# S5's loads of tables, G1, H and local kernels: issued on SyncE's queue instead of GpSimd's

## The chip, the core and the metric

The kernel runs on one core of a Trainium2 chip. Its engines are TensorE (PE: matmuls, and weight loads as PEld), VectorE (DVE), ScalarE (ACT), GpSimd (POOL) and SyncE (SP, which computes nothing and only issues transfers). Each engine works through its own list of instructions in order; a wait of one instruction holds all that stand behind it on that engine. Transfers between HBM and the core's memory (DMAs) go through queues, one for each issuing engine here, and are moved by 16 DMA engines. The metric is the time of one execution on the device in microseconds (us), lower is better.

## What is computed

A decoder trunk of two layers over 1024 positions with a width of 1024, in float32. The first layer's mixer is a gated DeltaNet; the second layer's is an S5 state-space layer: 64 groups of 16 channels each drive one complex state of 64 dimensions. Each mixer runs beside a cross-attention of 4 heads into 256 memory tokens, and an MLP follows. The change touches only the S5 layer:

```python
def s5_scan(u, abar_re, abar_im, bbar_re, bbar_im, c_re, c_im):
    """h_t = Abar h_{t-1} + Bbar u_t per group; y_t = Re(C h_t)."""
    ...
def s5_mixer(x, w_in, ...):
    u, xq = jnp.split(x @ w_in, [S5_DIM], axis=-1)
    ...
    y = s5_scan(u, abar_re, abar_im, bbar_re, bbar_im, c_re, c_im)
    y = y + d_skip * u
    zg = jax.nn.gelu(y)
    return zg * jax.nn.sigmoid(zg @ w_glu + b_glu), xq

def reference(x, mem, ...):
    for i in range(2):
        mix, xq = gdn_mixer(...) if i == 0 else s5_mixer(...)
        cross = memory_attention(xq, mem, w_kv_mem[i])
        x = layer_norm(DN_ALPHA * x + concatenate([mix, cross]) @ w_o[i])
        x = layer_norm(DN_ALPHA * x + square(relu(x @ mlp_w1[i])) @ mlp_w2[i])
```

## The kernel before

Float32 matmuls are made of three passes: an operand is split into a high part (a cast on ACT) and a low part (a subtraction on DVE), and `mm3` (L383 to L385) multiplies high by high, high by low and low by high. A weight therefore passes through three stations: `load_raw` (L351) loads it on SP into one of the two `raw` buffers, ACT casts it (L362), DVE subtracts (L363), and only then can TensorE use it. `wuh` and `wul` are the two parts of a weight of the S5 input `u`, `wur` its raw load; `wq`, `wv` and `wk` are the attention's weights in the same way. `mem_kv` (L1496) loads the memory tokens by the same raw buffers (`mem`), for the keys and values; ACT casts them at L1510.

The S5 front is the stretch of the second layer in which S5 runs, from about 1310 to 1640 us. It works on 8 rounds m of 8 groups each. A round has these steps:

- `s5_u` (L1967): the projection of the input onto 128 channels, from `xT` (`xTh`, `xTl`) and `wu`; the result is stored on SP to `ud` in HBM (L1978).
- `s5_driving` (L1986): the loads of a round's driving side, for each half round one `G1` (through `s5_load`, L1981) and two tables `tab` (L1997) of 256 KB each.
- `s5_drive` (L2015): loads `u` back from `ud` on SP (L2021), multiplies it by G1 on TensorE (`p1`), and turns and scans the product on DVE and ACT with the two tables; the result is `r`.
- `s5_reading` (L2002): the loads of the reading side: the local kernel `M0` (`s5_local`, L2008, 512 KB from `zd` into a quarter of the buffer `s5t`; the last round's, `ml`, has a buffer of its own and is loaded ahead of the front) and two `H` of 256 KB.
- `s5_read` (L2052): the products `py` of the local kernel with `u` (L2059) and of H with `r` (L2060), then ACT's GELU (`zg`), which SP stores to `yd` (L2063). The GLU reads `yd` after the front.

G1, H, the tables and the local kernels are made earlier, stored to HBM (`g1d`, `h1d`, `tabd`, `zd`), and come back in the front. In the kernel before, GpSimd issues all of these 72 loads: 32 tables, 16 G1, 16 H and 8 local kernels, 21 MB together. All other loads and stores of the front are issued by SP.

The order of the work in the front comes from a string of steps, one for K (keys and values of the memory), U (`s5_u`), D (`s5_drive` with the loads of the round after it and the reading loads of its own), R (`s5_read`), Q, S, T and V (the attention's queries, scores, transposes and values) and G (the GLU):

```python
    FRONT = "K K D0 K K U20 U21 R0 D1 K K U30 U31 R1 D2 K K Q00 U40 U41 R2 D3 Q01 S00 U50 U51 R3 D4 T00 V00 S01 ..."
```

At the end of the build a planner (`settle`, L58) puts all instructions of each engine into an order by estimated costs (`price`, L291; it takes an issue by POOL for dearer than one by SP) and fixes it. So a load that is moved to another engine can stand at another place among its neighbours than it was written at. Buffers come from pools with a fixed count by tag: two `raw`, nine `h2` (the tables), seven `h1` (G1, H and `r`). A load into a buffer waits until its last reader is done.

Each DMA signals its landing on a completion counter. The DMAs of SP use eight counters in turn, those of POOL eight others; a DMA waits until the DMA before it on its counter, the eighth before it on its queue, has landed.

Of the kernel before, what the change touches and what calls it, by code (L numbers as in the profile page):

```python
# [16 lines left out]
P = 128  # L17
# [13 lines left out]
class Trunk:  # L31
# [1948 lines left out]

    def s5_load(self, nm, tag, src):  # L1981
        t = self.tile(tag, [P, 4, P], F32, nm)
        self.nc.gpsimd.dma_start(t, src)
        return t

    def s5_driving(self, m):  # L1986

        out = []
        for b in range(2):
            gs = slice(4 * b, 4 * b + 4)  # L1990
            G1 = self.s5_load("G1", "h1", self.g1d[m, :, gs])
            c, q = (2 * m + b) % 8, m // 4
            tabs = []
            for x in range(2):
                t = self.tile("h2", [P, 4, P], F32, "tab")
                src = self.tabd[1:3, c, q] if x else self.tabd[0, c, q].unsqueeze(0).to_broadcast([2, 64, 4, P])
                self.nc.gpsimd.dma_start(t.rearrange("p g t -> p (g t)"), src.rearrange("k p g t -> k p (g t)"))  # L1997
                tabs.append(t)
            out.append((G1, tabs))
        return out  # L2000
# [7 lines left out]
    def s5_local(self, m, o):  # L2008

        M0 = o.rearrange("p (g x) -> p g x", g=8)  # L2010
        z = self.zd[m]
        self.nc.gpsimd.dma_start(M0, bass.AP(z.tensor, z.offset, [[16, 8], [8 * 240, 16], [240, 8], [1, P]]))
        return M0

    def s5_drive(self, m, loads):  # L2015
# [447 lines left out]
```

## Time and profile before

| what | value |
|---|---|
| time, median of 3 runs | 2501.77 us (2498.99, 2501.77, 2503.67) |
| time of the profiled execution | 2499.32 us |
| its span in the profile | 2497.3 us |
| its TensorE clock, mean granted | 0.998 |
| bytes by SP's queue (q1) | 372.50 MB, 46.9% of 16 engines' span |
| bytes by POOL's queue (q0) | 46.76 MB, 7.1% of 16 engines' span |

The page of the profile gives the busy time of each engine first, then a picture of the span in 40 slices of 62.4 us. These two of its rows show the busy share of TensorE and of the DMA engines in each slice, in tenths:

```profile
PE   9999999999999999999999999999999999999998
...
DMA  6445545566335665587455498884237544573422
```

The S5 front lies in the slices from the 22nd (which begins at 1311 us) to the 27th; the four that show DMA shares of 0.8 and 0.9 begin at 1436 us. A TensorE row is read as line, operation, output and inputs, tile, shape; the time in brackets behind it is how long the engine stood idle just before, and whose end released it. A row of a DMA issue gives the tile, the queue, the number of transfers and their size, and the median time from issue to landing.

### The profile page before, as it was taken

To read this page: it belongs to the slowest core of one execution; us is meant where nothing else is said; L and a number is where in the kernel's file an instruction comes from. 1 tells how busy PE (TensorE), PEld (TensorE's weight loads), DVE (VectorE), ACT (ScalarE), POOL (GpSimd) and SP (SyncE) were. 2 spreads that over 40 slices of the span, in tenths; PEclk is the share of its full clock that TensorE was granted. 3 is DMA by queue.
4 is the path that set the end of the run, shared out by engine and by line. 5 is a ranking of instruction groups with operands and counts; after the bars stand their busy time and mean duration, and the time that the engine had idled before them with its cause. 6 is when DMAs were issued, how large, how long until landed. Compare 5 with 4: busy or idle time off the path is not lost. (4 is left out here: it accounts for less than half of the span.)

```text
span 2497.3 us, 36513 instructions
## 1 busy us (share of the span) xinstructions
PE 2468.7 (99%) x12199; PEld 2056.2 (82%) x12199; DVE 1933.0 (77%) x3661; ACT 1387.5 (56%) x3114; POOL 275.4 (11%) x405
## 2 busy tenths in 40 slices
PE   9999999999999999999999999999999999999998
PEld 7888888888787888888888888888887888888886
DVE  7776868676889987879988856683988655587777
ACT  7766677665557576554444254672466555544444
POOL 1111111110001011312120122200010000000001
PEclk9999999999999999999999999999999999999999
DMA  6445545566335665587455498884237544573422
GB/s 206 131 114 155 153 137 141 150 194 200 109 116 184 212 222 185 177 281 252 136 171 156 139 238 223 198 265 143 77 118 239 173 162 148 205 277 105 148 89 97
DMA packets 304844, 426.17 MB, mean 171 GB/s; under 512 B 132832, under 2 KB 150192, under 8 KB 304656
## 3 DMA queue, kind: packets, MB, share of 16 engines
q1 hardware_dynamic: 270320, 372.50, 46.9%
q0 software_dynamic: 31744, 46.76, 7.1%
q10 hardware_dynamic: 2592, 4.59, 0.5%
q8 instruction: 96, 1.57, 0.3%
q14 instruction: 92, 0.75, 0.1%
HBM read 287.84 MB, written 135.76 MB: 170 GB/s over the span
## 5 line engine op out<-in xcount | busy, mean ns | idle before, releaser
L383 PE MATMUL q<-wkh,hkh 128*128 128x512 f32 x784 | 305.9, 390 | 0.0
L384 PE MATMUL q<-wkl,hkh 128*128 128x512 f32 x784 | 305.7, 390 | 0.0
L385 PE MATMUL q<-wkh,hkl 128*128 128x512 f32 x784 | 305.4, 390 | 0.0
L851 ACT CAST wkh<-wr 128x512 fp32r<-128x512 f32 x168 | 104.8, 624 | 233.2 <-PE q L384 153.6
L383 PEld LDWEIGHTS q<-wkh,hkh 128*128 128x128 f32 x784 | 147.2, 188 | 31.7 <-ACT wkh L851 1.0
L385 PEld LDWEIGHTS q<-wkh,hkl 128*128 128x128 f32 x784 | 147.2, 188 | 30.3
L384 PEld LDWEIGHTS q<-wkl,hkh 128*128 128x128 f32 x784 | 147.2, 188 | 30.3
L852 DVE TENSOR_TENSOR wkl<-wr,wkh 128x512 fp32r<-128x512 f32 x168 | 115.6, 688 | 63.7 <-issue 50.2
L383 PE MATMUL wi<-xTh,wih 128*128 128x512 f32 x376 | 152.0, 404 | 0.0
L384 PE MATMUL wi<-xTl,wih 128*128 128x512 f32 x376 | 150.0, 399 | 0.0
L385 PE MATMUL wi<-xTh,wil 128*128 128x512 f32 x376 | 149.9, 399 | 0.0
L506 POOL TENSOR_TENSOR mv<-mv,mhalf 128x1 f32<-128x1 f32 x32 | 29.5, 922 | 981.0 <-DVE mv L500 936.3
L852 DVE TENSOR_TENSOR hkl<-hr,hkh 128x512 fp32r<-128x512 f32 x196 | 134.0, 684 | 3.3 <-ACT hkh L851 3.3
L851 ACT CAST hkh<-hr 128x512 fp32r<-128x512 f32 x196 | 120.8, 616 | 4.6 <-DMA hr<-hd 4.6
L383 PE MATMUL o<-ow,ok 128*128 128x512 f32 x256 | 101.3, 396 | 1.0 <-ACT ok L1714 1.0
L385 PE MATMUL o<-ow,ok 128*128 128x512 f32 x256 | 101.3, 396 | 0.2
L384 PE MATMUL o<-ow,ok 128*128 128x512 f32 x256 | 100.0, 390 | 0.0
L844 DVE TENSOR_TENSOR y<-q,y 128x512 f32<-128x512 f32 x136 | 88.0, 681 | 0.0
L385 PEld LDWEIGHTS wi<-xTh,wil 128*128 128x128 f32 x376 | 70.8, 188 | 12.7
L383 PEld LDWEIGHTS wi<-xTh,wih 128*128 128x128 f32 x376 | 70.9, 189 | 11.8
L384 PEld LDWEIGHTS wi<-xTl,wih 128*128 128x128 f32 x376 | 71.0, 189 | 11.6
L1714 ACT CAST ok<-os 128x512 fp32r<-128x512 f32 x56 | 34.7, 621 | 53.3 <-PE o L385 39.1
(621 smaller groups left out, 7335.0 us busy)
## 6 DMA issues: line engine op xcount, KB each, us to landing
hr<-hd SPq DMA_DIRECT2D x212, 256.0 KB, 2.8
wr<-in_w_dram SPq DMA_DIRECT2D x56, 512.0 KB, 4.8
hd<-u SPq DMA_DIRECT2D x100, 256.0 KB, 2.2
w1r<-in_w_dram SPq DMA_DIRECT2D x48, 512.0 KB, 3.7
hd<-hid SPq DMA_DIRECT2D x60, 256.0 KB, 2.3
hd<-p SPq DMA_DIRECT2D x60, 256.0 KB, 2.6
w1r<-in_w_dram SPq DMA_DIRECT2D x48, 256.0 KB, 3.4
wir<-in_w_in_dram SPq DMA_DIRECT2D x23, 512.0 KB, 4.8
```

The costliest lines, as they stand in the source:

```text
L383: mm(ps, a[0], b[0], start=start, stop=False, skip_group_check=onto)
L384: mm(ps, a[0], b[1], start=False, stop=False, skip_group_check=onto)
L385: mm(ps, a[1], b[0], start=False, stop=stop, skip_group_check=onto)
L506: nc.gpsimd.tensor_tensor(mv[:, 3:4], mv[:, 2:3], self.mhalf[:, 0:1], op=ALU.pow)
L844: V.tensor_tensor(o, bank[t], o, op=ALU.add)
L851: nc.scalar.copy(hi, s)
L852: nc.vector.tensor_tensor(lo, s, f32(hi), op=ALU.subtract)
L1714: nc.scalar.copy(hi, s)
```

## The change

In three functions `dma_start` is called on `nc.sync` instead of `nc.gpsimd`. Sources, destinations, sizes and buffers are the same.

```diff
     def s5_load(self, nm, tag, src):
         t = self.tile(tag, [P, 4, P], F32, nm)
-        self.nc.gpsimd.dma_start(t, src)
+        self.nc.sync.dma_start(t, src)
         return t
...
     def s5_driving(self, m):
...
-                self.nc.gpsimd.dma_start(t.rearrange("p g t -> p (g t)"), src.rearrange("k p g t -> k p (g t)"))
+                self.nc.sync.dma_start(t.rearrange("p g t -> p (g t)"), src.rearrange("k p g t -> k p (g t)"))
...
     def s5_local(self, m, o):
...
-        self.nc.gpsimd.dma_start(M0, bass.AP(z.tensor, z.offset, [[16, 8], [8 * 240, 16], [240, 8], [1, P]]))
+        self.nc.sync.dma_start(M0, bass.AP(z.tensor, z.offset, [[16, 8], [8 * 240, 16], [240, 8], [1, P]]))
```

The orders of TensorE, VectorE and ScalarE are the same in both kernels. POOL's list is 72 rows shorter, SP's 72 rows longer, and the planner chose where on SP each load stands. Three places of SP's list follow; a row with + is a load that came from POOL, a row without a sign stood there before (source line, output and input, shape; numbers behind a name tell buffers apart).

The first is ahead of the second load of memory tokens (`mem_14936`), at 1416 us, while SP stores and loads rows of `x` for the layer's end. The tables are those of the first three rounds:

```order
 L2366 DMA x_6957<-y_11552 128x1024 x2
+L1997 DMA tab_15017<-tabd 128x1x512
+L1997 DMA tab_15021<-tabd 128x1x512
+L1997 DMA tab_15023<-tabd 128x1x512
+L1997 DMA tab_15072<-tabd 128x1x512
+L1997 DMA tab_15074<-tabd 128x1x512
+L1997 DMA tab_15078<-tabd 128x1x512
+L1997 DMA tab_15080<-tabd 128x1x512
+L1997 DMA tab_15283<-tabd 128x1x512
+L1983 DMA G_2867_15019<-g1d 128x512
 L353 DMA mem_14936<-in_memT_dram 128x1024
```

Nine loads, eight tables and a G1, now stand between the stores of `x` and `mem_14936`, which stood right behind each other.

The second is at 1469 us, between two attention weights (`wvr_15481` and `wvr_15499`). The loads that came are those of the reading side of one round (local kernel and two H) and two G1 of the next:

```order
 L353 DMA wvr_15481<-in_wv_dram 128x1024
+L2012 DMA s5t_14779<-zd 128x8x128
 L2063 DMA yd<-zg_15221 128x512
 L2063 DMA yd<-zg_15233 128x512
+L1983 DMA G_2911_15281<-g1d 128x512
+L1983 DMA G_2914_15287<-g1d 128x512
+L1983 DMA H_2917_15294<-h1d 128x4x128
+L1983 DMA H_2918_15296<-h1d 128x4x128
 L2021 DMA s5t_14779<-ud 128x1024
 L353 DMA wvr_15499<-in_wv_dram 128x1024
```

Five loads now stand ahead of the second attention weight, and the local kernel stands ahead of the two stores of `yd`.

The third follows right behind it (from 1477 us on), up to the loads of the next round. `wqr_15521` is an attention weight, `wur_15556` the weight of `u` of round 4:

```order
 L353 DMA wvr_15499<-in_wv_dram 128x1024
+L1997 DMA tab_15468<-tabd 128x1x512
+L1997 DMA tab_15472<-tabd 128x1x512
+L1997 DMA tab_15474<-tabd 128x1x512
+L1997 DMA tab_15686<-tabd 128x1x512
 L353 DMA wqr_15521<-in_w_in_dram 128x1024
 L1978 DMA ud<-s5t_14779 128x8x128
 L353 DMA wur_15556<-in_w_in_dram 128x1024
 L2063 DMA yd<-zg_15404 128x512
+L2012 DMA s5t_14779<-zd 128x8x128
 L2063 DMA yd<-zg_15416 128x512
+L1983 DMA G_2944_15464<-g1d 128x512
```

Four tables now stand ahead of `wqr` and `wur`; the next round's local kernel, G1 and H stand behind `wur`.

## The prediction

> **What bounds the kernel now.** I read the page's busy times first.
>
> ```profile
> span 2497.3 us, 36513 instructions
> ...
> PE 2468.7 (99%) x12199; PEld 2056.2 (82%) x12199; DVE 1933.0 (77%) x3661; ACT 1387.5 (56%) x3114; POOL 275.4 (11%) x405
> ```
>
> TensorE is busy for 2468.7 of 2497.3 us, so at most 28.6 us of its idle time can be won anywhere. The order of PE, DVE and ACT is unchanged, so the change acts only through when data arrive. The next view is who TensorE waits for between 1360 and 1700 us, where the S5 front runs (line, releaser: us in total, times, longest).
>
> ```profile
> PE wu L383 <- ACT wuh L362: 1.4, 1, 1.4
> ...
> PE wu L383 <- ACT xTh L534: 0.7, 1, 0.7
> PE wu L385 <- DVE wul L363: 0.5, 1, 0.5
> ...
> PE wu L384 <- DVE xTl L535: 0.2, 1, 0.2
> ```
>
> Two places stand out. The first, in order of time of TensorE (start, duration, idle before), is this:
>
> ```profile
> 1504.23 0.39 PE L384 MATMUL wq<-xTl,wqh 128*128 128x512 f32 x1
> 1504.45 0.39 PE L385 MATMUL wq<-xTh,wql 128*128 128x512 f32 x1
> 1506.27 0.50 PE L383 MATMUL wu<-xTh,wuh 128*128 128x512 f32 x1 [1.43 <-ACT wuh L362]
> ...
> 1507.53 0.75 PE L385 MATMUL wu<-xTh,wul 128*128 128x512 f32 x1 [0.52 <-DVE wul L363]
> 1508.08 0.63 PE L383 MATMUL wu<-xTh,wuh 128*128 128x512 f32 x1
> ...
> 1511.29 0.40 PE L385 MATMUL wu<-xTh,wul 128*128 128x512 f32 x1
> 1511.52 0.40 PE L383 MATMUL wu<-xTh,wuh 128*128 128x512 f32 x1
> ```
>
> Matmuls follow each other every 0.22 to 0.23 us at full pace (1504.23 to 1504.45, 1511.29 to 1511.52). From 1504.45 to 1511.29 twelve of these steps take 6.84 us where 12 x 0.227 = 2.72 would do: **4.1 us lost**, half by waiting, half because matmuls behind the wait run at 0.63 us. Why it waited, on ACT and DVE:
>
> ```profile
> 1505.17 1.04 ACT L362 CAST wuh<-wur 128x1024 fp32r<-128x1024 f32 x1 [6.50 <-DMA wur<-in_w_in_dram]
> ...
> 1506.25 1.22 DVE L363 TENSOR_TENSOR wul<-wur,wuh 128x1024 fp32r<-128x1024 f32 x1 [5.35 <-ACT wuh L362]
> ```
>
> A weight load of SP landed late. ACT stood for it for 6.50 us. At full pace TensorE would want `wuh` at 1504.68 and `wul` at 1505.13; `wul` was ready at 1507.47. So that load must land 2.4 us earlier, by about 1502.7, for the whole loss to go.
>
> The second place is at 1430: 0.7 + 0.2 us behind ACT's `xTh`. On ACT:
>
> ```profile
> 1428.15 1.14 ACT L1510 CAST memh<-mem 128x512 fp32r<-128x512 f32 x2 [3.06 <-DMA mem<-in_memT_dram]
> ...
> 1429.67 1.07 ACT L534 CAST xTh<-xt 128x512 fp32r<-128x512 f32 x2
> ```
>
> ACT takes its work in order, and 3.06 us went by on another load of SP (`mem`) just ahead.
>
> **Why those loads are late.** I compare how fast the two issuing paths move data: first while POOL's loads have the DMA engines alone, second SP's alone but for the last 2 us, third both (stretch, ..., granted clock, DMA share, GB/s), with each stretch's main queue (packets, MB) below.
>
> ```profile
> 1413.00:1419.00 6.00, 6.00 (x28) 4.98 (x27) 5.09 (x9) 0.00 (x0) 5.62 (x8) 1.00 0.54 98
> 1439.00:1450.00 11.00, 11.00 (x84) 10.49 (x83) 3.33 (x5) 4.51 (x8) 1.67 (x2) 1.00 0.92 286
> 1470.00:1506.00 36.00, 34.84 (x189) 29.79 (x187) 19.62 (x34) 15.61 (x24) 11.17 (x14) 1.00 1.02 255
> ```
>
> ```profile
> q0 software_dynamic: 1786, 0.57, 53.1%
> q1 hardware_dynamic: 2647, 3.13, 91.8%
> ```
>
> POOL's queue (q0) gets 98 GB/s out of engines that nobody else uses; SP's (q1) gets 286. Together they move 255 with the engines full. So the loads that the change moves are the slow ones, and they hold up SP's. By the page, issue to landing (median us):
>
> ```profile
> tab<-tabd POOLq DMA_DIRECT2D x32, 256.0 KB, 11.9
> ...
> G<-g1d POOLq DMA_DIRECT2D x16, 256.0 KB, 12.5
> ...
> H<-h1d POOLq DMA_DIRECT2D x16, 256.0 KB, 13.4
> ...
> s5t<-zd POOLq DMA_DIRECT2D x7, 512.0 KB, 12.5
> ```
>
> **The change part by part.** 32 tables, 16 G1, 16 H and 8 local kernels (64 x 256 + 8 x 512 KB, 21 MB) leave POOL for SP. What an issue costs on POOL (ns, min/median/max), and SP's own issues between 1469 and 1495 us, in order of time:
>
> ```profile
> L1997 POOL DMA_DIRECT2D tab<-tabd x32: 787/816/866, 1367.9 to 1585.2; - x32
> ```
>
> ```profile
> 1469.08 0.39 SPq L353 DMA_DIRECT2D wvr<-in_wv_dram  x1
> 1470.21 1.24 SPq L2063 DMA_DIRECT2D yd<-zg  x2
> ...
> 1477.17 0.33 SPq L353 DMA_DIRECT2D wvr<-in_wv_dram  x1
> 1484.37 0.33 SPq L353 DMA_DIRECT2D wqr<-in_w_in_dram  x1
> ...
> 1493.39 0.33 SPq L353 DMA_DIRECT2D wur<-in_w_in_dram  x1
> 1493.77 1.81 SPq L2063 DMA_DIRECT2D yd<-zg  x1
> ```
>
> *Issuing.* POOL sheds 72 issues of about 0.8 us; TensorE never waits on POOL there, so that is worth 0. SP gains 72 issues of 0.33 us, 24 us, or of 1.81 us, 130 us, if every one went as slowly as the last row. They are spread over the 300 us from 1310 to 1610, in which SP mostly waits: 0 either way, unless a wait of a moved load holds up what stands behind it.
>
> *New waits on SP.* Two kinds move to SP, seen on POOL now:
>
> ```profile
> 1310.06 1.36 POOL L2012 DMA_DIRECT2D ml<-zd  x1 [1.05 <-DVE wr L787]
> ...
> 1470.90 1.32 POOL L2012 DMA_DIRECT2D s5t<-zd  x1 [7.35 <-PE py L2060]
> ```
>
> The first local kernel is free to go by 1310.1. Behind it on SP stand `hr` and second-layer weights whose casts come later than 1326; a hold of a microsecond costs nothing. The others wait for TensorE's reading product; the one shown is free by 1470.9, 0.7 us after the `yd` store that now stands behind it (1470.21) and 6 us ahead of the next weights (1477.17). Nobody reads `yd` before the GLU: 0. The four tables ahead of `wqr` now were issued on POOL between 1479.6 and 1483.7 us, so their buffers were free before `wqr`'s 1484.37: 0. SP's DMAs also share eight completion counters where POOL's had eight more, so a DMA can wait for the eighth before it: `wvr` of 1477.17 would wait for the local kernel, at worst (by the sum below) until 1478.4 + 0.52 MB / 255 GB/s = 1480.5. By then over 2 MB stand in the queue ahead of it, so it lands no later: 0.
>
> *The wait at 1506.* One queue serves in order. At 1469.1 + 9.3 = 1478.4 the first `wvr` has landed (row below). Suppose nothing issued after it has moved by then, the worst case. Through the late `wur` the new order (shown above) holds the local kernel 512 KB, two `yd` stores 512, G1 512, H 512, u 512, `wvr` 512, four tables 1024, `wqr` 512, the `ud` store 512, `wur` 512: 5632 KB, 5.77 MB. At SP's 286 GB/s that is 20.2 us, 1498.6; at today's mixed 255 it is 22.6 us, 1501.0.
>
> ```profile
> wvr<-in_wv_dram SPq DMA_DIRECT2D x1, 512.0 KB, 9.3
> ...
> wur<-in_w_in_dram SPq DMA_DIRECT2D x1, 512.0 KB, 11.7
> ```
>
> Today it lands at 1493.4 + 11.7 = 1505.1. Both ends meet 1502.7, since the next local kernel, G1 and H, which compete with it now, stand behind it. I take the whole **-4.1 us** (bounds -4.1 and 0).
>
> *The wait at 1430.* `mem` (issued 1416.24) gets nine moved loads ahead of it, 2.36 MB, and is 0.52 MB. At 286 GB/s from 1413 that is 10.1 us, 1423; ACT then needs no wait, but `xTh` still follows TensorE's transposes. I take half of 0.93: **-0.5 us** (bounds -0.9 and, at POOL's pace, the slower rival below).
>
> *The moved loads' own users.* The tightest is H, issued at 1474.1:
>
> ```profile
> H<-h1d POOLq DMA_DIRECT2D x1, 256.0 KB, 14.6
> ...
> 1490.43 0.39 PE L2060 MATMUL py<-r,H 128*128 128x127 f32 x2
> ```
>
> It lands at 1488.7, 1.7 us ahead of use. In one queue, 2048 KB from 1478.4 at 255 GB/s end at 1486.6 or sooner: 0.
>
> Sum: -4.6 us on the profiled execution's 2499.32 (span 2497.3), so 2494.7. That execution is 2.4 us under the median of the three runs, 2501.77; the same gain from it gives **2497.2**.
>
> **What the Trainium skill says of it.** *DMA: Bandwidth & Descriptors*, section "Issuing engines are not separate DMA queues", states that all issuers' DMAs run on the same 16 engines and that the issuing engine is a matter of sequencer time only; by it the sum is 0. The 98 against 286 GB/s above speak against it here. The same page, "Queues, rings and completion order", states that an engine alternates between queues packet by packet; by it SP's loads lose the half share that they had beside POOL's, the mechanism of the slower rival.
>
> **The rivals.**
> - *No change, or the idle time turns up elsewhere.* The transport stays as slow, or TensorE, 4 us ahead, meets the next late load. For: the engines show full use (1.02). Against: both ends of the sum above. About 2501.8.
> - *More goes.* The other short waits of the stage go too, and the runs of 2501.77 and 2503.67 us have more of them than the profiled one. 4.1 + 0.9 + 2 for what separates that execution from the median: -7, 2494.8.
> - *Slower: `mem` behind nine loads.* If the pace of 98 GB/s belongs to these loads' shapes and not to POOL's queue, the 2.88 MB through `mem` take 29.4 us from 1413, to 1442. ACT stands in front of it with `xTh` behind, so TensorE stands from 1430: +14 us, 2516. It decides from about 194 GB/s (2.88 MB in the 14.9 us to 1428.1, when ACT gets it now). Against: SP moves its own loads at 286.
> - *The change doesn't do what it says*: the order excludes it.
>
> **How the numbers follow.** Forecast 0.55, more 0.18, no change 0.20, slower 0.07. A measurement of this kernel tells about 0.2%, 5.0 us, from no change. The forecast's 4.6 us lies just inside; of its 0.55 I count 0.20 beyond 5.0. Faster 0.20 + 0.18 = 0.38; same 0.35 + 0.20 = 0.55; slower 0.07. Range: from 2493.5 (the larger gain and a little) to 2502.0 (no gain), which leaves out the slower case and the tails.
>
> **What would show it.** `wuh` gone from TensorE's waits, and no 0.63 us matmuls behind it; q0 at 25.8 MB, q1 at 393.5; tables, G1 and H landing in 3 to 9 us; `mem` gone from ACT's waits. Wrong, if moved loads land on SP as late as on POOL, or if TensorE shows a new wait on `xTh`, `wqh` or `wuh`.

## The result, and the profile after

The changed kernel takes 2587.5 us (median of 5 runs, 2585.24 to 2587.78) where the kernel before, on the same chip, takes 2500.97 us (median of 5, 2498.55 to 2503.67): a ratio of **1.0343**, 95% interval 1.0329 to 1.0357. It is 86 us slower; the forecast was 4.6 us faster.

From the page of the changed kernel: span, busy times, TensorE's granted clock by slice, and the two queues.

```profile
span 2585.8 us, 36473 instructions
...
PE 2486.1 (96%) x12199; PEld 2066.4 (80%) x12199; DVE 1934.0 (75%) x3661; ACT 1390.0 (54%) x3114; POOL 222.0 (9%) x333
...
PEclk9999999999999999999999788899999999999999
...
q1 hardware_dynamic: 293488, 393.47, 47.4%
q0 software_dynamic: 10112, 25.64, 3.1%
```

The 21 MB did move to SP's queue (q1 from 372.50 to 393.47 MB). TensorE's idle time went from 28.6 us (2497.3 less 2468.7) to 99.7 us (2585.8 less 2486.1), 71.1 us more, and its busy time grew by 17.4 us though it does the same work: the slices of the front, from the 23rd on, show a granted clock of 0.7 to 0.8. Together 88.5 us, the whole difference of the two spans.

What TensorE waits for from 1250 to 1750 us, in the changed kernel (line, releaser: us in total, times, longest):

```profile
PE wu L383 <- ACT xTh L534: 30.8, 1, 30.8
PE wu L383 <- ACT wuh L362: 11.6, 1, 11.6
PE wq L383 <- ACT wqh L362: 10.5, 1, 10.5
PE py L2060 <- DMA H<-h1d: 9.7, 4, 2.7
PE py L2059 <- DMA s5t<-zd: 7.7, 4, 3.8
```

The longest wait is the one at 1430 us that was 0.7 us before. It is followed back through ACT (start, duration, idle before) and then SP's issues, both of the changed kernel in order of time:

```profile
1459.08 1.14 ACT L1510 CAST memh<-mem 128x512 fp32r<-128x512 f32 x2 [33.66 <-DMA mem<-in_memT_dram]
1460.12 0.58 ACT L1972 COPY s5t<-wu 128x512 f32<-128x512 f32 x1
1460.60 1.07 ACT L534 CAST xTh<-xt 128x512 fp32r<-128x512 f32 x2
```

```profile
1411.99 30.86 SPq L1997 DMA_DIRECT2D tab<-tabd  x8
1442.94 4.92 SPq L1983 DMA_DIRECT2D G<-g1d  x1
1447.97 0.46 SPq L353 DMA_DIRECT2D mem<-in_memT_dram  x1
```

`xTh` is late because ACT first stands 33.66 us for `mem`. `mem` is late because SP issues it at 1447.97 where it was issued at 1416.24 before, and SP is late because eight tables ahead of it took 30.86 us to issue. What the DMA engines did meanwhile (windows of the changed kernel: stretch, busy times, granted clock, DMA share, GB/s; then the queue's packets, MB and share from 1416 to 1446 us):

```profile
1416.00:1446.00 30.00, 14.43 (x72) 11.90 (x70) 9.92 (x14) 2.70 (x5) 1.96 (x2) 0.81 0.13 51
1500.00:1510.00 10.00, 10.00 (x68) 9.04 (x66) 4.66 (x7) 5.71 (x9) 0.00 (x0) 1.00 0.13 51
1534.00:1545.00 11.00, 11.00 (x75) 10.01 (x74) 4.65 (x7) 5.05 (x8) 0.00 (x0) 1.00 0.13 51
...
1556.00:1558.00 2.00, 0.97 (x2) 0.50 (x2) 0.99 (x1) 1.46 (x2) 0.00 (x0) 0.50 0.54 163
```

```profile
q1 hardware_dynamic: 761, 1.53, 13.1%
```

**While tables move, the share is 13% of 16 engines: two engines**, and 51 GB/s, again and again (1416, 1500 and 1534 us). Nothing else is queued that could use the other fourteen, since SP's list stands. A table of 262,144 bytes takes 5.1 us at that pace, and a table's issue takes as long once those before it fill the two engines: the operation row of the tables, by GpSimd 816 ns in the middle, is now

```profile
L1997 SPq DMA_DIRECT2D tab<-tabd x32: 502/3116/7113, 1368.9 to 1669.4; - x32
```

The source of a table's load counts two in its slowest dimension (two blocks of 64 rows, or one block taken twice); that of a local kernel counts eight, and around 1556 us, while a local kernel moves, the share is 0.54, near eight or nine engines. G1, H and the weights count 128. That makes a theory, called SPREAD below: on SP's queue a load is moved by no more engines than its slowest dimension counts.

The Trainium skill, *DMA: Bandwidth & Descriptors*, section "Why a DMA increments its semaphore by 16 and not by 1", states this as a rule: as many engines, up to 16, as divide the slowest dimension larger than one of both sides. By it a table gets two, a local kernel eight and G1 16. The shares of 0.13 and 0.54 agree.

### The profile page after: what moved, and what is told of

Its sections match the earlier page's. It is cut to its first block, busy times and chain, and to the rows that moved or that the text cites. A ratio compares the mean times of both kernels' runs of the same rounds, so it can differ in the third digit from the quotient of the medians.

```text
span 2585.8 us, 36473 instructions
## 1 busy us (share of the span) xinstructions
PE 2486.1 (96%) x12199; PEld 2066.4 (80%) x12199; DVE 1934.0 (75%) x3661; ACT 1390.0 (54%) x3114; POOL 222.0 (9%) x333
## 3 DMA queue, kind: packets, MB, share of 16 engines
q1 hardware_dynamic: 293488, 393.47, 47.4%
## 5 line engine op out<-in xcount | busy, mean ns | idle before, releaser
L383 PE MATMUL wu<-xTh,wuh 128*128 128x512 f32 x128 | 52.0, 406 | 42.4 <-ACT xTh L534 30.8
```

Of the source, the lines that this page charges most:

```text
L383: mm(ps, a[0], b[0], start=start, stop=False, skip_group_check=onto)
```

## The experiments

The rival to SPREAD is ORDER: nine loads ahead of `mem`, and four tables ahead of weights, are too much for one queue however they are spread.

**Row halves.** Each table by two DMAs of 64 rows; nothing else changes, and TensorE, VectorE, ScalarE and GpSimd keep the changed kernel's order.

```diff
-                src = self.tabd[1:3, c, q] if x else self.tabd[0, c, q].unsqueeze(0).to_broadcast([2, 64, 4, P])
-                self.nc.sync.dma_start(t.rearrange("p g t -> p (g t)"), src.rearrange("k p g t -> k p (g t)"))
+                for k in range(2):
+                    self.nc.sync.dma_start(t[64 * k:64 * k + 64], self.tabd[(1 + k) * x, c, q])
```

> The changed kernel, with each table loaded by two DMAs of 64 rows instead of one DMA whose slowest dimension counts two (two halves of 64 rows each). Same bytes, same queue, same order of the loads; the orders of TensorE, VectorE, ScalarE and GpSimd are the same as in the changed kernel. Theory SPREAD (a load whose slowest dimension counts two is moved by two of the 16 DMA engines on SyncE's queue, at 51 GB/s as the trace of the changed kernel shows from 1416 to 1448 us, and all behind it in the queue waits): the waits of 30.8, 11.6 and 10.5 us go, no stretch with 51 GB/s remains, and the time is 2494 to 2506 us. Theory ORDER (nine loads ahead of mem_14936, and tables ahead of wqr and wur, on one queue are too much however they are spread): TensorE still waits more than 10 us on xTh at about 1430 us, and the time is above 2560 us.

Measured: 2495.68 us (median of 11, before 2500.51), ratio 0.9982, interval 0.9974 to 0.9991. The waits of TensorE in the front, SP's issues ahead of `mem`, and a window with tables moving, of this kernel:

```profile
PE pv L383 <- ACT pTh L1592: 1.1, 2, 0.9
PE mk L385 <- DVE wkl L363: 0.4, 1, 0.4
PE wu L383 <- ACT xTh L534: 0.3, 1, 0.3
```

```profile
1414.35 7.01 SPq L1997 DMA_DIRECT2D tab<-tabd  x10
1421.44 0.54 SPq L1983 DMA_DIRECT2D G<-g1d  x1
1422.03 1.72 SPq L1997 DMA_DIRECT2D tab<-tabd  x3
1423.86 0.52 SPq L353 DMA_DIRECT2D mem<-in_memT_dram  x1
```

```profile
1416.00:1424.00 8.00, 8.00 (x37) 6.63 (x36) 7.49 (x13) 0.00 (x0) 1.41 (x1) 1.00 0.71 211
1424.00:1432.00 8.00, 8.00 (x42) 6.68 (x42) 6.07 (x9) 3.90 (x8) 0.55 (x1) 1.00 0.95 311
```

The same queue and the same bytes: 211 to 311 GB/s instead of 51, and no long wait. The order is nearly the same: 13 of the 16 half tables and the G1 are issued ahead of `mem`, three half tables behind it. SPREAD is met; ORDER falls.

**Column halves**, the control: also two DMAs of 128 KB for each table, but cut along the columns, so that each still counts two.

```diff
-                self.nc.sync.dma_start(t.rearrange("p g t -> p (g t)"), src.rearrange("k p g t -> k p (g t)"))
+                for g in range(2):
+                    self.nc.sync.dma_start(t[:, 2 * g:2 * g + 2].rearrange("p g t -> p (g t)"), src[:, :, 2 * g:2 * g + 2].rearrange("k p g t -> k p (g t)"))
```

> The control for the kernel above: each table also by two DMAs of 128 KB, but cut along the columns, so that the slowest dimension of each still counts two. Theory SPREAD: as slow as the changed kernel or slower (rows of 1 KB instead of 2 KB on the same two engines), 2575 to 2680 us, with long stretches of two DMA engines busy. Theory SIZE (what helps is that a DMA is half as large, or that a table has two completion counters): as fast as the row halves, 2494 to 2506 us.

Measured: 2584.19 us (2 runs), ratio 1.0334 (1.0316 to 1.0352). A window of it while tables move ahead of `mem`:

```profile
1417.00:1434.00 17.00, 12.06 (x62) 9.95 (x60) 7.99 (x13) 2.70 (x5) 0.55 (x1) 0.97 0.14 48
```

Two engines still, 48 GB/s, and SIZE falls. So it is not the size of a DMA or the number of them that the row halves cured. What is left is the pattern: a source of two blocks against one of 64 rows. That the count of blocks sets the number of engines rests on two points, the tables at two and the local kernel at eight.

**Tables only**: that part of the change alone, the other two functions as before.

```diff
-                self.nc.gpsimd.dma_start(t.rearrange("p g t -> p (g t)"), src.rearrange("k p g t -> k p (g t)"))
+                self.nc.sync.dma_start(t.rearrange("p g t -> p (g t)"), src.rearrange("k p g t -> k p (g t)"))
```

> One part of the change alone: the 32 tables on SyncE, as in the changed kernel; G1, H and local kernels back on GpSimd. Theory SPREAD: the three long waits of 53 us together stay, and the time is 2560 to 2590 us; the waits of the reading products on local kernels and H (17.4 us together in the changed kernel) shrink, since those loads no longer stand behind tables on SyncE. Theory ORDER: fewer loads share the queue, so the loss falls in proportion to the bytes (32 tables are 8.4 of 21 MB): about 2500 + 0.4 x 87 = 2535 us.

Measured: 2595.06 us (4 runs), ratio 1.0377 (1.0364 to 1.0390). The loss is the tables', and alone they are even 8 us slower than the whole change, above the expected 2560 to 2590. The first waits in the front:

```profile
PE wu L383 <- ACT xTh L534: 31.3, 1, 31.3
PE wu L383 <- ACT wuh L362: 16.7, 1, 16.7
PE wq L383 <- ACT wqh L362: 12.1, 1, 12.1
PE p L2034 <- DMA H<-h1d: 11.5, 1, 11.5
PE p L2034 <- DMA s5t<-ud: 6.0, 1, 6.0
```

The waits of the reading products did go, as expected, but driving products now wait 17.5 us. They read `u` and G1, whatever load the row names. The longer wait ends at 1683.39 us, just after two G1 have landed that GpSimd issued from 1673.32 us on (9.2 us to landing). They were that late because GpSimd's list had stood 14.55 us for the buffer of an H and 12.53 us for that of a local kernel. Four tables took SP 19.73 us to issue there (from 1637.45 us) where the changed kernel needs 12 to 14. That GpSimd's loads beside them are the reason is likely but not shown.

**All but the tables**: G1, H and local kernels on SP as in the changed kernel, the tables back on GpSimd.

```diff
-                self.nc.sync.dma_start(t.rearrange("p g t -> p (g t)"), src.rearrange("k p g t -> k p (g t)"))
+                self.nc.gpsimd.dma_start(t.rearrange("p g t -> p (g t)"), src.rearrange("k p g t -> k p (g t)"))
```

> The other part alone: G1, H and local kernels on SyncE, the tables back on GpSimd. Theory SPREAD: no 51 GB/s stretch on SyncE's queue and no long wait; 2492 to 2506 us, with the wait of 1506 us of the kernel before gone or not. Theory ORDER: 60% of the bytes remain, about 2500 + 0.6 x 87 = 2552 us.

Measured: 2497.39 us (median of 12, before 2500.51), ratio 0.9990 (0.9982 to 0.9999). The two longest waits of TensorE in the front, of this kernel:

```profile
PE pv L383 <- ACT pTh L1592: 1.1, 2, 0.9
PE mk L385 <- DVE wkl L363: 0.4, 1, 0.4
```

No wait on `wuh` is left here either, and none of the loss. ORDER, which wanted 2552, falls a second time.

**Row halves for the first rounds only**: are the waits worth what each shows?

```diff
+                if m <= 2:
+                    for k in range(2):
+                        self.nc.sync.dma_start(t[64 * k:64 * k + 64], self.tabd[(1 + k) * x, c, q])
+                else:
                     self.nc.sync.dma_start(t.rearrange("p g t -> p (g t)"), src.rearrange("k p g t -> k p (g t)"))
```

> The changed kernel with the row halves for the tables of rounds 0 to 2 alone (all nine loads ahead of mem_14936, and three of the four ahead of the weight whose late cast makes the wait of 11.6 us); rounds 3 to 7 load their tables as the changed kernel does. Theory ADDITIVE (each late load costs by itself): the waits of 30.8 and 11.6 us go but for about 0.7 us, and with them the half granted clock behind them (14.9 and 13.7 us of work at half pace, 14 us): 2587.5 - 41.7 - 14 = 2532 us, between 2525 and 2542. Theory CATCH-UP (while TensorE stood in the first wait the queue got ahead, so without that wait the later ones grow by the same): above 2560 us.

Measured: 2539.24 us (2 runs), ratio 1.0147 (1.0126 to 1.0167): 48 us of the 86 are gone, 7 fewer than the sum of 56, inside the range. The idle part of the sum held: TensorE's idle time fell from 99.7 to 55.0 us (2537.4 less 2482.4), 44.7 us. The clock part did not: its busy time fell from 2486.1 to 2482.4 us, 3.7 us where the sum had 14. In the changed kernel the granted clock is 0.5 for only about 5 us of work behind each of the two waits (1461 to 1466 and 1522 to 1527 us). What is left in the front:

```profile
PE wq L383 <- ACT wqh L362: 11.0, 1, 11.0
PE py L2064 <- DMA H<-h1d: 9.8, 4, 2.7
PE py L2063 <- DMA s5t<-zd: 5.7, 4, 3.5
```

These were 10.5, 9.7 and 7.7 us: the later waits stay about as they were. ADDITIVE holds for the waits, and nothing is caught up.

**Row halves on GpSimd**: the kernel before with its tables cut into rows, nothing moved to another queue. This tests the ground of the forecast, that GpSimd's queue is slow by itself. The order of TensorE is the same; ScalarE and VectorE run a few operations between 1417 and 1430 us in another order.

```diff
-                src = self.tabd[1:3, c, q] if x else self.tabd[0, c, q].unsqueeze(0).to_broadcast([2, 64, 4, P])
-                self.nc.gpsimd.dma_start(t.rearrange("p g t -> p (g t)"), src.rearrange("k p g t -> k p (g t)"))
+                for k in range(2):
+                    self.nc.gpsimd.dma_start(t[64 * k:64 * k + 64], self.tabd[(1 + k) * x, c, q])
```

> The kernel before, with each table loaded by two DMAs of 64 rows, all still issued by GpSimd. Theory QUEUE (GpSimd's queue is slow by itself, 98 GB/s in the trace of the kernel before, whatever the shape): tables land no sooner than 8 us after issue, the stretch of GpSimd's loads alone moves 80 to 130 GB/s, and the time is 2496 to 2506 us. Theory SHAPE (it was the two-row pattern that made GpSimd's loads slow too): over 200 GB/s there, landings of 3 to 6 us, the wait at 1506 us gone, 2490 to 2498 us.

Measured: 2497.25 us (median of 10, before 2501.46), ratio 0.9985 (0.9975 to 0.9994). A window with GpSimd's loads almost alone, first of the kernel before, then of this one, and the issues of this one with their landings over the front (tile, queue, count, size, median us):

```profile
1415.00:1419.00 4.00, 4.00 (x19) 3.34 (x18) 3.09 (x5) 0.00 (x0) 3.62 (x6) 1.00 0.62 126
```

```profile
1415.00:1419.00 4.00, 4.00 (x20) 3.30 (x19) 4.00 (x6) 0.00 (x0) 3.75 (x7) 1.00 0.79 239
```

```profile
tab<-tabd POOLq DMA_DIRECT2D x64, 128.0 KB, 6.8
...
G<-g1d POOLq DMA_DIRECT2D x16, 256.0 KB, 12.6
...
H<-h1d POOLq DMA_DIRECT2D x16, 256.0 KB, 14.3
```

In the same four microseconds GpSimd's queue moves 239 GB/s once the tables' pattern is gone, where it moved 126 (98 from 1413 to 1419 us, the prediction's row). TensorE's wait at 1506 us is gone too: its longest wait in the front is 0.9 us. SHAPE is right on what matters, and QUEUE falls. Not all fits SHAPE: tables land in 6.8 us, not 3 to 6, and G1 and H land as late as before (12.5 and 13.4 us), while on SP, in the run with row halves, they take 7.2 and 6.9 us.

**Local kernels in eight**: the row halves on SP, and each local kernel by eight DMAs of 16 rows.

```diff
-        self.nc.sync.dma_start(M0, bass.AP(z.tensor, z.offset, [[16, 8], [8 * 240, 16], [240, 8], [1, P]]))
+        for s in range(8):
+            self.nc.sync.dma_start(M0[16 * s:16 * s + 16], bass.AP(z.tensor, z.offset + 16 * s, [[8 * 240, 16], [240, 8], [1, P]]))
```

> The row halves, and each local kernel too by eight DMAs of 16 rows (its one DMA has a slowest dimension of eight; 8 to 9 packets are in flight when it moves alone in the trace of the changed kernel). Theory SPREAD: the local kernels move on all 16 engines, but no reading product waits for one in the run with row halves, so nothing is won: 2491 to 2501 us. Theory ISSUE (56 more issues on SyncE delay the weights behind them): a new wait on a weight's cast, above 2502 us.

Measured: 2496.50 us (median of 10, before 2501.46), ratio 0.9978 (0.9968 to 0.9987): no different from the row halves alone, 0.9982, within their intervals. No new wait on a weight's cast came, so ISSUE falls. G1 and H land sooner, in 4.7 and 5.7 us (medians) where the row halves alone have 7.2 and 6.9. Nobody waits for them, so it is worth nothing. The three kernels with row halves for all tables, at 0.9978 to 0.9985, beat both kernels of this study by a little, and cannot be told from each other.

## Why the prediction was wrong, step by step

- *What bounds the kernel.* Right: TensorE, and only the arrival of data could move the time. The bound of 28.6 us on what can be won said nothing of what can be lost.
- *"POOL's queue (q0) gets 98 GB/s out of engines that nobody else uses; SP's (q1) gets 286."* **The step that failed.** The two rows compared two queues carrying different loads: tables mainly on one, weights and `u` on the other. The difference was put down to the queue. With the tables' pattern taken out, GpSimd's queue moved 239 GB/s; with it, SP's moved 51. The 98 was no steady pace either, but the mean of a queue that was just starting (the kernel before, two microseconds each):

```profile
1413.00:1415.00 2.00, 2.00 (x11) 1.65 (x10) 2.00 (x6) 0.00 (x0) 2.00 (x3) 1.00 0.39 42
1415.00:1417.00 2.00, 2.00 (x10) 1.67 (x9) 1.18 (x2) 0.00 (x0) 2.00 (x5) 1.00 0.45 95
1417.00:1419.00 2.00, 2.00 (x10) 1.67 (x9) 1.91 (x3) 0.00 (x0) 1.62 (x3) 1.00 0.79 157
```

A sign of the pattern stood in the prediction's own rows: 0.57 MB in 1786 packets is 0.3 KB a packet, SP's 3.13 MB in 2647 is 1.2 KB.

- *"At 286 GB/s from 1413 that is 10.1 us, 1423"* for `mem` behind nine loads. This carried SP's pace for weights over to loads that SP had never carried. `mem` was issued at 1447.97 and ACT had it at 1459.08; TensorE stood 30.8 us.
- *Issuing: "0 either way".* The bound of 1.81 us for one issue came from a store of `yd`; a table's issue took 3.1 us in the middle and up to 7.1. "SP mostly waits" hid nothing, since these issues come in runs, ahead of loads that ACT waits for.
- *The wait at 1506, -4.1 us.* It went, even in the changed kernel. The twelve steps that took 6.84 us take 2.72 there, and 2.72 with row halves (first and last matmul; the changed kernel, then row halves):

```profile
1564.52 0.39 PE L385 MATMUL wq<-xTh,wql 128*128 128x512 f32 x1
1567.24 0.39 PE L385 MATMUL wu<-xTh,wul 128*128 128x512 f32 x1
```

```profile
1507.16 0.39 PE L385 MATMUL wq<-xTh,wql 128*128 128x512 f32 x1
1509.88 0.39 PE L385 MATMUL wu<-xTh,wul 128*128 128x512 f32 x1
```

In the changed kernel it drowned: `wuh` of an earlier weight costs 11.6 us (at 1521.94) and `wqh` 10.5 (at 1557.03), just ahead. The same wait also goes when the tables stay on GpSimd in row halves, and when all but the tables move, so moving the tables to SP was not needed for it. Which load had made that weight late is not singled out.

- *The wait at 1430, -0.5 us.* In the changed kernel it grew to 30.8 us. With row halves `xTh` and `xTl` cost 0.5 us where they cost 0.93.
- *The sum, -4.6 us.* With row halves the median is 4.8 us under the kernel before. That the two agree so well is in part luck: the profiled execution with row halves gained both terms in the front, but it had come to the front about 3 us later (the product of 1430.31 starts at 1433.07 there), and its span, 2497.4 us, is that of the kernel before, 2497.3.
- *What would show it wrong.* The prediction named a new wait on `xTh`, `wqh` or `wuh`. All three came.
- *The moved loads' own users: 0.* Wrong in the changed kernel: 17.4 us on local kernels and H, which are issued behind tables. With row halves no such wait is left.
- *The slower rival.* Its place was right, TensorE stands from 1430 us behind `mem`, and so was its mechanism in the main: the pace goes with the loads' shapes, though on SP it was lower still than on GpSimd. Its condition, below 194 GB/s, was met by far. Its size was wrong: 14 us, from GpSimd's 98 GB/s as the worst pace, against 30.8 us at 51, and it had only one of the places. Its chance of 0.07 rested on "SP moves its own loads at 286", a row of loads of another pattern, which was no evidence on it. The patterns stood in the code: two blocks of 64 rows against 128 rows.

## What to carry to other kernels

Before a load is moved between queues, read its pattern: a row of the profile gives the pace of a queue *with the loads it carries*, a mean over its start is lower than what it reaches, and the same load can run at another pace on another queue. On SP's queue here a load was moved by two engines where its source's slowest dimension counts two; cut it first so that both sides count more (64 in the row halves), and only then compare queues. And a slow load on a shared queue is paid by whatever stands behind it: look at what is next on that queue, not at the load's own users.

## What the runs showed of the hardware that was not expected

- An issue on SP is not a fixed 0.33 us: behind tables on two engines single issues took 5 us, also that of a G1, whose slowest dimension counts 128 (4.92 us at 1442.94, against 0.54 us in the run with row halves).
- On GpSimd's queue the tables' pattern cost packets. The rows of the kernel before, and of the same kernel with row halves (packets, MB, share):

```profile
q0 software_dynamic: 31744, 46.76, 7.1%
```

```profile
q0 software_dynamic: 17920, 46.65, 6.8%
```

That is 13,824 packets and 0.11 MB fewer. By the sizes in the two traces, 14,336 packets of 8 bytes are gone, 448 for each of the 32 tables, and 512 of 4 bytes are new, 16 for each of the 32 DMAs more. What those of 8 bytes are for stays open; that the loads are faster without them is measured, that they are the cause is not.
